# Dilated projections in natural token order, and the tiles of split products at one place modulo 256 bytes

## The chip, the cores and the metric

One Trainium2 chip; the kernel uses one of its cores. The metric is the device time of one execution in microseconds (us). A core has a matrix engine (PE; its weight loads, PEld, overlap its matmuls), a vector engine (DVE), an activation engine (ACT), a general engine (POOL) and a sync engine (SP) that issues every DMA of this kernel in order. On-chip memory is SBUF; matmuls write to PSUM.

## The reference, cut to what matters

Two networks run in sequence on 512 tokens of 1024 features in float32. The first is a mixer with two gated linear attentions followed by a PEER layer: top-k retrieval over 16384 experts, computed here densely as `gelu(u x)`, gates, and a product with `v`. The second has two layers; each is half a feed-forward block, a mixer, and another half:

```
swiglu_half: h = rms_norm(x, g);  (silu(h @ w_gate) * (h @ w_up)) @ w_down       # 1024 -> 2816 -> 1024
ab mixer:    z = rms_norm(x) @ ab_w_in; concat(mla_mixer(z), dilated_mixer(z)) @ ab_w_out
dilated_mixer(z): for g, (w, d) in enumerate(((128, 1), (512, 4), (2048, 16))):  # 4 heads of 64 per group
    q, k = qk_norm(zq_g), qk_norm(zk_g);  v = zv_g
    # to_res: tokens r, r+d, r+2d, ... form a sequence of their own
    o_g, lse_g = banded_attention(to_res(q), to_res(k), to_res(v), w // d + 1, bias, dist_scale=d)
  out = sum_g softmax_g(lse_g) * o_g
```

Groups 1 and 2 attend within residue classes of the token index (the kernel uses four classes for both; for `d = 16` its bias table masks what is not in the same class of 16).

## The kernel before, in words

Activations `x` lie feature-major: eight tiles of 128 features x 512 tokens. Nearly every large product is a *split product*. Both operands are split into a rounded high part and a low remainder in fp32r, and three matmuls accumulate high*high, high*low, low*high (`mm3`, L248 to L251). Weights are streamed: SP loads a `wst` tile of 128 x 1024 (four buffers), ACT writes the high part `whi`, DVE the low part `wlo` (`gran`, L213; three buffers of each). In feature-major products the weight block is the stationary operand and 512 tokens of the activation split are the moving one: names `gu` (gate and up), `dn` (down), `ua` and `qa` (PEER), `pacc` (PEER output), `fl`, `br`, `wo`, `mo`. In token-major products (`pj`, `vps`, `gps`) it is the other way round: 128 tokens of the activation split are stationary and 256 weight columns move (`project`, L1145).

The split activations are `xgh`/`xgl` in the second network, `hfh`/`hfl` into `dn`, `ph`/`pl` into `ua` and `qa`, `ag` into `pacc`, `mth`/`mtl` into `mo` of the ab mixer, `mt` into `mo` of the other mixer. Where a tile starts follows from the sizes of what was put in its pool before it; sizes are rounded to 32 bytes.

**ab mixer** (about 3009 to 3370 us). `mixer_ab` (L1194) makes twelve half projections F0 to F11: q, k, v of groups 1 and 2, each over 1024 x 256 weights, each half with two blocks of 128 tokens. Each block is 24 matmuls, so groups 1 and 2 have 6 x 4 x 24 = 576. Their tokens are taken with step 4, `s.st4 = [slice(i, 512, 4) ...]` (L1200), so that block `i` holds residue class `i`. The F pieces stand between the steps of `mla` (L1218): T0 to T7 (project, normalise and rotate one token block for four heads: PE `qb`, `kvb`, then ACT, POOL, DVE on tile `mx`, then PE transposes) and U0 to U7 (attention units: PE `lg`, DVE and ACT softmax, PE `tr`, `ob`). Then `dilated` (L1338): H0 to H2 normalise q and k of a group on DVE and transpose them (`dqT`, `dkT`, evicted by ACT), D are the attention units, E the projections of group 0 in natural order, O the output product `mo`. A scheduler fixes each engine's order when the program is built; the written order is its starting point.

Of the kernel before, what the change touches and what calls it, by code (L numbers as in the profile page):

```python
# [9 lines left out]
F32 = mybir.dt.float32  # L10
F32R = mybir.dt.float32r
F16 = mybir.dt.float16
I32 = mybir.dt.int32
# [140 lines left out]
    return {k: np.ascontiguousarray(v) for k, v in out.items()}  # L154


class Net:
    SQT = ("P", 2), ("L", 4)

    def __init__(s, ctx, tc, A, out, upto=None, dbg=None):  # L160
        s.ctx, s.tc, s.nc, s.A, s.out = ctx, tc, tc.nc, A, out
        s.upto, s.dbg = upto, dbg or {}
        s.hi_dve = False
        s.unnormed = False
        s.WB, s.NST = 3, 4
        nc = s.nc
        s.V, s.S, s.G, s.T = nc.vector, nc.scalar, nc.gpsimd, nc.tensor
        s.c = ctx.enter_context(tc.tile_pool(name="consts", bufs=1, reuse_waits="tile"))
        s.wp = ctx.enter_context(tc.tile_pool(name="weights", bufs=1, reuse_waits="tile"))
        s.dr = ctx.enter_context(tc.tile_pool(name="dram", bufs=1, space=DRAM))  # L170
        s.consts()

# [26 lines left out]
    def consts(s):  # L199
        c, V, G, A = s.c, s.V, s.G, s.A  # L200
        s.ones = c.tile([128, 128], F32, name="ones")
        V.memset(s.ones[:], 1.0)
        ii = c.tile([128, 128], I32, name="ii")
        G.iota(ii[:], pattern=[[1, 128]], base=0, channel_multiplier=-1)
        s.ident = c.tile([128, 128], F32, name="ident")
        s.ts(s.ident[:], ii[:], 0.0, None, ALU.is_equal)

        s.shift = c.tile([128, 128], F32, name="shift")
        s.ts(s.shift[:], ii[:], -1.0, None, ALU.is_equal)
        s.vecs = c.tile([128, 72], F32, name="vecs")  # L210
        s.load(s.vecs[:], A["vecs"])

    def gran(s, src):  # L213

# [140 lines left out]
    def first(s):  # L355
        tc, A, c = s.tc, s.A, s.c
        s.ysp = s.dr.tile([16, 128, 512], F32, name="ysp")
        with ExitStack() as es:
            s.ps = es.enter_context(s.psum(3, 1))
            hp = es.enter_context(tc.tile_pool(name="hpool", bufs=1, reuse_waits="tile"))  # L360
            with ExitStack() as e1:
                p = e1.enter_context(tc.tile_pool(name="adap", bufs=1, reuse_waits="tile"))
                s.ada_first(p, hp)()
            s.sgp = es.enter_context(tc.tile_pool(name="sgp", bufs=1, reuse_waits="tile"))
            with ExitStack() as e1:
                wk = e1.enter_context(tc.tile_pool(name="gla", bufs=1, reuse_waits="tile"))
                s.gla_setup(wk)
                for j in range(4):
                    s.hg_pair(wk, j)
                    if j == 0:  # L370
                        s.bias_skew()
                for h in range(4):
                    s.gla_head(wk, h)
                sgs = [s.merge_gate(m) for m in range(2)]
            mp = es.enter_context(tc.tile_pool(name="ymp", bufs=1, reuse_waits="tile"))
            with ExitStack() as e1:
                ym = s.merge(e1.enter_context(tc.tile_pool(name="merge", bufs=1, reuse_waits="tile")), mp, sgs)
            s.xp = s.ctx.enter_context(tc.tile_pool(name="xres", bufs=1, side="right", reuse_waits="tile"))
            s.mix_out(ym)

# [392 lines left out]
    def peer(s):  # L773
        tc, A = s.tc, s.A

        s.gd = [s.dr.tile([32, 128, 512], F32, name=f"gd{q}") for q in range(4)]
        s.ad = s.dr.tile([128, 128, 512], F32, name="ad")
        acc = s.sumsq_w(s.x)
        with tc.tile_pool(name="peer", bufs=1, reuse_waits="tile") as p:
            s.peer_u(p, acc)  # L780
            s.peer_v(p)

# [216 lines left out]
    def norm_in(s, gain):  # L999

        if not hasattr(s, "sb"):

            s.sb = s.ctx.enter_context(s.tc.tile_pool(name="second", bufs=1, reuse_waits="tile"))
        return [s.split(s.sb, s.x[k][:], "xg", 8, scale=gain[:, k:k + 1]) for k in range(8)]

    def norm_rs(s, p, views):
# [25 lines left out]
    def ffn(s, l, f):  # L1032
        A = s.A
        wgu, wd = A[f"wgu{l}{f}"], A[f"wd{l}{f}"]
        with ExitStack() as es:
            s.ps = es.enter_context(s.psum(6, 1))
            col = (24 if f == 1 else 56) + 8 * l
            gain = s.vecs[:, col:col + 8]
            if s.unnormed:
                s.tt(gain, gain, s.vecs[:, 16:24], ALU.mult)  # L1040
            xg = s.norm_in(gain)
            p = es.enter_context(s.tc.tile_pool(name="ffn", bufs=1, reuse_waits="tile"))
            nat = [slice(128 * i, 128 * i + 128) for i in range(4)]
            if s.unnormed:
                Rb = s.norm_twice(p, nat)
            else:
                Rb = s.bcast(p, s.norm_rs(p, nat))
            for half in range(2):
                H = []
                for m in range(11):  # L1050
                    pp = []
                    for e in range(2):
                        a = s.mm_ps("gu")
                        s.prod(a[:], s.gran(wgu[11 * half + m, e]), xg)
                        pp.append(a)
# [138 lines left out]
    def mixer_ab(s):  # L1194
        with ExitStack() as es:
            s.ps = es.enter_context(s.psum(3, 2))
            xg = s.norm_in(s.vecs[:, 40:48])
            p = es.enter_context(s.tc.tile_pool(name="ab", bufs=1, reuse_waits="tile"))
            s.nat = [slice(128 * i, 128 * i + 128) for i in range(4)]
            s.st4 = [slice(i, 512, 4) for i in range(4)]  # L1200
            R = s.norm_rs(p, s.nat + s.st4)
            mixed = p.tile([128, 4, 768], F32, name="mixed")
            s.dx = {}
            fill = [f for g in (1, 2) for n in range(3) for f in s.dil_proj(p, xg, R, g, n)]
# [5 lines left out]
    def dil_proj(s, p, xg, R, g, n):  # L1210

        def dst(i):
            if (g, n) not in s.dx:
                s.dx[g, n] = p.tile([128, 4, 4, 64], F32, tag="dx", bufs=6, name="dx")
            return s.dx[g, n][:, i].rearrange("p h d -> p (h d)")
        return s.halves(s.A["ab_d"][3 * g + n], xg, s.st4 if g else s.nat, R[:, 4:8] if g else R[:, 0:4], 256, dst)

    def mla(s, p, up, xg, R, mixed, fill):  # L1218
        A, V = s.A, s.V
# [22 lines left out]

        cm = p.tile([128, 512], F32, name="cm")
        V.memset(cm[:, :384], 0.0)
        gtm = p.tile([128, 128], I32, name="gtm")
        s.G.iota(gtm[:], pattern=[[1, 128]], base=0, channel_multiplier=-1)
        s.ts(cm[:, 384:], gtm[:], 0.0, BIG, ALU.is_gt, ALU.mult)

        ss = p.tile([128, 4, 2], F32, name="ss2")
        for i in range(4):  # L1250
# [72 lines left out]
        for n in order[order.index("Z") + 1:]:  # L1323
            pc[n]()

    def qk_heads(s, p, x, R_, nh, gain, neg, dst):


        for i in range(4):
# [3 lines left out]
            s.tt(x[:, i], x[:, i], r[:, :, None].to_broadcast([128, nh, 64]), ALU.mult)  # L1333
        for j in range(nh // 2):
            pt = s.transpose4([x[:, i, 2 * j:2 * j + 2, :].rearrange("p h d -> p (h d)") for i in range(4)])
            s.act(dst[j][:], pt[:], AF.Copy, scale=gain)

    def dilated(s, p, up, xg, R, mixed):  # L1338
        A, V = s.A, s.V
        hg = p.tile([128, 8], F32, name="hdg")  # L1340
        s.load(hg[:], A["hd_g"])
        perm = s.dr.tile([2, 512, 272], F32, name="perm")
        bias = [s.bias_tile(p, f"dil{g}") for g in range(3)]
        mt = [s.to_feat(p, mixed, k) for k in range(4)]
# [2 lines left out]
        def heads(g):  # L1347
            qT = [p.tile([128, 512], F32, tag="dqT", bufs=4, name="dqT") for _ in range(2)]
            kT = [p.tile([128, 512], F32, tag="dkT", bufs=4, name="dkT") for _ in range(2)]
            s.qk_heads(up, s.dx[g, 0], None, 4, hg[:, 0:1], -0.125, qT)  # L1350
            s.qk_heads(up, s.dx[g, 1], None, 4, hg[:, 1:2], None, kT)
            return qT, kT

        def units(g, i, qT, kT):
# [67 lines left out]
    def mixer_cd(s):  # L1422
        A = s.A
        with ExitStack() as es:
# [3 lines left out]
            nat = [slice(128 * i, 128 * i + 128) for i in range(4)]  # L1428
            R = s.norm_rs(p, nat)
            mixed = p.tile([128, 4, 1024], F32, name="mixed")  # L1430
            hg = p.tile([128, 8], F32, name="hdg")
            s.load(hg[:], A["hd_g"])
            flat = lambda t, i: t[:, i].rearrange("p h d -> p (h d)")

            def proj(n, t):
# [294 lines left out]
```

## Time and profile before

| | us |
|---|---|
| median of 3 runs (4804.04 to 4808.37) | 4805.89 |
| the profiled execution | 4807.03 |
| its span on the core | 4805.3 |
| PE busy in the span | 4691.8 |

The stages of the span: first mixer to 1014 us, PEER `ua` 1026 to 1918 and `pacc` 1918 to 2636, feed-forward halves 2638 to 3009, ab mixer to about 3370, two more halves to 4099, the other mixer to about 4430, the last half to 4805. A matmul's shown duration is longer than its step to the next one, since matmuls are pipelined: the step is read from starts. A busy share says nothing of how long each step is.

### The profile page before, as it was taken

The numbers are of one execution on the slowest core, as the hardware profiler recorded it, in microseconds if no ns is written. First come the engines' busy times: TensorE is split into PE (matmuls) and PEld (weight loads), VectorE is DVE, ScalarE is ACT, GpSimd is POOL, SyncE is SP. The second block draws the span as 40 slices with busy tenths as digits, with TensorE's granted clock in tenths as the row PEclk, the third lists the DMA queues.
The fourth block names the chain that finished last, engine by engine and source line by source line (L and its number), as shares of the span: only waits on it lengthen the run. The fifth ranks groups of instructions, "written<-read, shape, count | busy, mean of one in ns | idle before, by whom it ended". The sixth has DMA issues, their size and how long they took to land.

```text
span 4805.3 us, 61237 instructions
## 1 busy us (share of the span) xinstructions
PE 4691.8 (98%) x23805; PEld 3874.1 (81%) x23805; DVE 2535.3 (53%) x5117; ACT 1753.1 (36%) x3150; POOL 228.6 (5%) x204
## 2 busy tenths in 40 slices
PE   7999998999999999999999999999999999999999
PEld 5898886878888887888887888988788888966887
DVE  4655555568866553444445634356544544555443
ACT  3444344232345444222223323345323323354322
POOL 1000000000000000000000100010100100000100
PEclk8999899999999999999999999999999999999999
DMA  7222113433356667666665233211333333211332
GB/s 209 66 64 70 53 53 103 147 123 126 121 169 195 178 193 215 187 188 187 190 187 168 86 98 89 68 34 51 116 98 96 93 96 97 80 40 42 95 98 84
DMA packets 320655, 559.17 MB, mean 116 GB/s; under 512 B 153883, under 2 KB 163995, under 8 KB 320364
## 3 DMA queue, kind: packets, MB, share of 16 engines
q1 hardware_dynamic: 320364, 555.26, 38.5%
q8 instruction: 186, 3.05, 0.3%
q14 instruction: 105, 0.86, 0.1%
HBM read 480.58 MB, written 80.62 MB: 117 GB/s over the span
## 4 chain that ended last, share of the span: by engine, by line
PE 93%; DVE 2%; ACT 2%; DMA 2%; issue 1%; SPq 0%; DVEq 0%; ACTq 0%
PE gu L250 7%; PE gu L251 7%; PE gu L249 7%; PE ua L249 5%; PE ua L251 5%; PE ua L250 5%; PE pacc L249 5%; PE pacc L251 5%; PE pacc L250 5%; PE dn L251 3%; PE dn L250 3%; PE dn L249 3%; PE pj L249 2%; PE pj L250 2%; PE pj L251 2%; PE lg L1132 2%
## 5 line engine op out<-in xcount | busy, mean ns | idle before, releaser
L185 ACT ACTIVATE whi<-wst 128x1024 fp32r<-128x1024 f32 (+3 forms) x720 | 737.1, 1024 | 1529.9 <-issue 355.1
L188 DVE TENSOR_TENSOR wlo<-wst,whi 128x1024 fp32r<-128x1024 f32 (+3 forms) x720 | 945.1, 1313 | 615.9 <-ACT whi L185 592.8
L249 PE MATMUL gu<-xgh,whi 128*128 128x512 f32 x1408 | 549.4, 391 | 9.4 <-DVE x L188 7.2
L250 PE MATMUL gu<-xgl,whi 128*128 128x512 f32 x1408 | 550.0, 391 | 1.0 <-DVE xgl L197 1.0
L251 PE MATMUL gu<-xgh,wlo 128*128 128x512 f32 x1408 | 549.5, 390 | 0.0
L249 PE MATMUL ua<-ph,whi 128*128 128x512 f32 x1024 | 409.8, 400 | 2.2 <-ACT ph L185 2.2
L251 PE MATMUL ua<-ph,wlo 128*128 128x512 f32 x1024 | 407.0, 397 | 0.0
L250 PE MATMUL ua<-pl,whi 128*128 128x512 f32 x1024 | 406.4, 397 | 0.0
L249 PE MATMUL pacc<-ag,whi 128*128 128x512 f32 x1024 | 404.6, 395 | 0.7 <-ACT ge L185 0.7
L251 PE MATMUL pacc<-ag,wlo 128*128 128x512 f32 x1024 | 404.5, 395 | 0.0
L250 PE MATMUL pacc<-ag,whi 128*128 128x512 f32 x1024 | 404.5, 395 | 0.0
L188 DVE TENSOR_TENSOR t<-gu,Rb 128x512 f32<-128x512 f32 x176 | 120.7, 691 | 391.0 <-PE gu L251 384.5
L249 PEld LDWEIGHTS gu<-xgh,whi 128*128 128x128 f32 x1408 | 265.3, 188 | 66.0 <-issue 5.7
L250 PEld LDWEIGHTS gu<-xgl,whi 128*128 128x128 f32 x1408 | 265.2, 188 | 56.9 <-DVE xgl L197 1.9
L251 PEld LDWEIGHTS gu<-xgh,wlo 128*128 128x128 f32 x1408 | 265.3, 188 | 54.6
L249 PE MATMUL dn<-hfh,whi 128*128 128x512 f32 x704 | 277.6, 394 | 0.0
L251 PE MATMUL dn<-hfh,wlo 128*128 128x512 f32 x704 | 276.3, 394 | 0.0
L250 PE MATMUL dn<-hfl,whi 128*128 128x512 f32 x704 | 276.3, 394 | 0.0
L1061 POOL TENSOR_TENSOR t<-t,t 128x512 f32<-128x512 f32 x88 | 123.9, 1409 | 3108.2 <-ACT t L185 2116.2
L185 ACT ACTIVATE ag<-ga 128x512 fp32r<-128x512 f32 x128 | 80.9, 632 | 507.5 <-PE pacc L250 507.2
L249 PEld LDWEIGHTS pacc<-ag,whi 128*128 128x128 f32 x1024 | 191.9, 187 | 48.1 <-ACT ge L185 1.2
L251 PEld LDWEIGHTS pacc<-ag,wlo 128*128 128x128 f32 x1024 | 191.9, 187 | 47.0
(503 smaller groups left out, 9042.5 us busy)
## 6 DMA issues: line engine op xcount, KB each, us to landing
wst<-in_wgu_dram SPq DMA_DIRECT2D x176, 512.0 KB, 3.5
wst<-in_u_dram SPq DMA_DIRECT2D x128, 512.0 KB, 3.7
wst<-in_v_dram SPq DMA_DIRECT2D x128, 512.0 KB, 3.6
ad<-ge SPq DMA_DIRECT2D x128, 256.0 KB, 2.0
ga<-ad SPq DMA_DIRECT2D x128, 256.0 KB, 2.6
gd<-gst SPq DMA_DIRECT2D x32, 1024.0 KB, 11.4
gq<-gd SPq DMA_DIRECT2D x128, 256.0 KB, 3.0
wst<-in_wd_dram SPq DMA_DIRECT2D x64, 448.0 KB, 3.3
```

The lines of the kernel that those rows point to most:

```text
L185: s.S.activation(out, in_, f, **kw)
L188: s.V.tensor_tensor(out, a, b, op)
L249: s.T.matmul(ps, a[0], b[0], start=start, stop=False)
L250: s.T.matmul(ps, a[0], b[1], start=False, stop=False)
L251: s.T.matmul(ps, a[1], b[0], start=False, stop=stop)
L1061: s.G.tensor_tensor(u[:], u[:], t[:], ALU.mult)
L1132: s.T.matmul(lp[:, :n], q, k, start=True, stop=True)
```

## The change

**Order of tokens.** The projections of groups 1 and 2 now take 128 neighbouring tokens (`s.nat`) and the statistics of four token slices instead of eight. q and k are put into residue order when ACT evicts their transposes: it reads PSUM with a step of four elements. v is put into residue order by a round trip: `dx` is stored to the DRAM tile `vperm` and loaded back as four runs of 1 KB per partition.

**Places.** `Lines` wraps a tile pool and rounds each tile's size up to 128 or 256 bytes. Most pools with operands of split products are wrapped. Three small tiles go: `ii` borrows a weight buffer, `gtm` is written into `cm`, `hdg` becomes eight more columns of `vecs`, loaded at the start. In the built programs the tiles start here, in bytes modulo 256:

| operand | before | after |
|---|---|---|
| `whi`, `wlo` (weights); `xgh`, `xgl`; all activation splits of the first mixer; `mt` | 96 | 128 |
| `ph`, `pl` (`ua`, `qa`: 3456 matmuls) | 64 | 128 |
| `ag` (`pacc`: 3072) | 128 | 128 |
| `hfh`, `hfl` (`dn`: 2112) | 32, some 128 | 128 |
| `mth`, `mtl` (`mo` of the ab mixer: 144) | 0 | 128 |

Before, 8784 matmuls of these four rows have their operands at different places, and some 9800 at the same one (96 and 96).

```
class Lines:
    def tile(s, shape, dt, **kw):
        n, size = math.prod(shape[1:]), s.BYTES[dt]
        if n * size % s.unit == 0:
            return s.pool.tile(shape, dt, **kw)
        t = s.pool.tile([shape[0], -(-n * size // s.unit) * s.unit // size], dt, **kw)[:, :n]
        ...
-        s.wp = ctx.enter_context(tc.tile_pool(name="weights", bufs=1, reuse_waits="tile"))
+        s.wp = Lines(ctx.enter_context(tc.tile_pool(name="weights", bufs=1, reuse_waits="tile")))
...
-            s.st4 = [slice(i, 512, 4) for i in range(4)]
-            R = s.norm_rs(p, s.nat + s.st4)
+            R = s.norm_rs(p, s.nat)
+            s.vperm = s.dr.tile([2, 512, 256], F32, name="vperm")
...
-        return s.halves(s.A["ab_d"][3 * g + n], xg, s.st4 if g else s.nat, R[:, 4:8] if g else R[:, 0:4], 256, dst)
+        h = s.halves(s.A["ab_d"][3 * g + n], xg, s.nat, R, 256, dst)
+        if g == 0 or n < 2:
+            return h
+
+        def last():
+
+            h[1]()
+            x = s.dx[g, n][:].rearrange("p i h d -> p i (h d)")
+            s.store(s.vperm[g - 1].rearrange("(i p) c -> p i c", p=128), x)
+            s.load(x, s.vperm[g - 1].rearrange("(p r) c -> p r c", r=4))
+        return [h[0], last]
...
+            if residues:
+                s.act(dst[j][:].rearrange("p (r a) -> p r a", r=4), pt[:].rearrange("p (a r) -> p r a", r=4), AF.Copy, scale=gain)
```

The order of instructions on PE, DVE, ACT and POOL hardly changes (a few neighbours swap). Two places differ. On the SP queue, in the ab mixer before (`in_ab_d` are the dilated weights, `in_ab_o` the output weights, `b_dil` the bias tiles, `hdg` the gains):

```order
L175 DMA wst<-in_ab_d_dram 128x1024 x10
L175 DMA wst<-in_ab_o_dram 128x512
L175 DMA wst<-in_ab_d_dram 128x1024 x4
L175 DMA wst<-in_ab_o_dram 128x512
L175 DMA wst<-in_ab_d_dram 128x1024
L175 DMA hdg<-in_hd_g_dram 128x8
L175 DMA b_dil_26121<-sk_dil_1440 128x4x256
```

and now, the same stretch of the SP queue:

```order
L193 DMA wst<-in_ab_d_dram 128x1024 x10
L196 DMA vperm<-dx 128x4x256
L193 DMA wst<-in_ab_o_dram 128x512
L193 DMA dx<-vperm 128x1024
L193 DMA wst<-in_ab_d_dram 128x1024 x4
L196 DMA vperm<-dx 128x4x256
L193 DMA wst<-in_ab_o_dram 128x512
L193 DMA wst<-in_ab_d_dram 128x1024
L193 DMA dx<-vperm 128x1024
L193 DMA b_dil_26120<-sk_dil_1441 128x4x256
```

Each group's v is stored and loaded back, with one or two weight loads between; the bias tiles come behind the second load, and the load of `hdg` has gone to the start of the program.

On PE, between the first projections of the ab mixer, the statistics matmuls before:

```order
L249 MATMUL pj<-whi,xgh 128x256
L250 MATMUL pj<-wlo,xgh 128x256
L321 MATMUL st<-ones,acc 128x1 x8
L251 MATMUL pj<-whi,xgl 128x256
L249 MATMUL pj<-whi,xgh 128x256
```

and now:

```order
L268 MATMUL pj<-whi,xgh 128x256
L269 MATMUL pj<-wlo,xgh 128x256
L340 MATMUL st<-ones,acc 128x1 x4
L270 MATMUL pj<-whi,xgl 128x256
L268 MATMUL pj<-whi,xgh 128x256
```

Four of the eight go; the projections around them stand as they stood.

## Rows read from the trace of the kernel before

**Rows 1.** the page: span, part 1, part 4's shares of the chain

```profile
span 4805.3 us, 61237 instructions
PE 4691.8 (98%) x23805; PEld 3874.1 (81%) x23805; DVE 2535.3 (53%) x5117; ACT 1753.1 (36%) x3150; POOL 228.6 (5%) x204
PE 93%; DVE 2%; ACT 2%; DMA 2%; issue 1%; SPq 0%; DVEq 0%; ACTq 0%
```

**Rows 2.** windows of tiles `gu` and `dn`: window, length, PE busy (matmuls), granted clock

```profile
3917.82:4037.52 119.70, 119.70 (x528) 1.00 0.31 96
...
4037.52:4098.88 61.36, 61.36 (x263) 1.00 0.33 95
```

**Rows 3.** windows of tiles `ua` and `pacc`, the same columns

```profile
1873.58:1918.46 44.88, 44.88 (x192) 1.00 0.93 271
...
1918.46:2636.03 717.57, 716.82 (x3071) 1.00 0.63 185
```

**Rows 4.** tile `mo`: count, shortest/median/longest ns, first and last start us

```profile
L249 PE MATMUL mo<-mt,whi x64: 389/393/774, 4273.6 to 4428.4; 128*128 128x512 f32 x64
L249 PE MATMUL mo<-mth,whi x48: 389/400/793, 3242.0 to 3366.5; 128*128 128x512 f32 x48
```

**Rows 5.** timeline, PE: gate projection `gz`, whose stationary operand has 24 columns

```profile
4182.04 0.39 PE L249 MATMUL gz<-xgh,whi 128*24 128x512 f32 x1
...
4184.57 0.39 PE L251 MATMUL gz<-xgh,wlo 128*24 128x512 f32 x1
```

**Rows 6.** projections `pj`: timeline (start us, us, line, form), then the tile's weight loads

```profile
3049.30 0.40 PE L249 MATMUL pj<-whi,xgh 128*128 128x256 f32 x1
...
3060.50 0.38 PE L351 MATMUL tr<-ident,za 128*128 128x128 f32 x2
...
L249 PEld LDWEIGHTS pj<-whi,xgh x16: 329/329/329, 3049.2 to 3059.7; 128*128 128x128 f32 x16
```

**Rows 7.** `pj`, 3020 to 3025.8: window (length, PE, PEld busy, count), weight loads

```profile
3020.00:3025.80 5.80, 5.76 (x48) 5.76 (x49) 0.37 (x1) 1.96 (x5) 0.00 (x0) 1.00 0.02 3
...
L249 PEld LDWEIGHTS pj<-whi,xgh x17: 186/192/192, 3020.0 to 3025.8; 128*128 128x128 f32 x17
```

**Rows 8.** timeline, ACT: one plain 128-column eviction

```profile
3187.05 0.28 ACT L185 ACTIVATE P<-tr 128x128 f32<-128x128 f32 x1 [3.37 <-PE tr L1138]
```

**Rows 9.** tile `dqT`: its ACT evictions from PSUM

```profile
L185 ACT ACTIVATE dqT<-tr,hdg x6: 678/684/692, 3247.1 to 3315.7; 128x512 f32<-128x512 f32 x6
```

**Rows 10.** tile `st`: statistics matmuls of this stage, from 3014 to 3018

```profile
L321 PE MATMUL st<-ones,acc x16: 168/310/372, 3014.4 to 3016.8; 128*128 128x1 f32 x16
```

**Rows 11.** windows: length, then PE, PEld, DVE, ACT, POOL busy us (count)

```profile
1100.00:1200.00 100.00, 99.33 (x453) 80.95 (x452) 84.82 (x349) 29.49 (x40) 0.00 (x0) 1.00 0.38 124
3029.00:3231.00 202.00, 200.26 (x981) 185.65 (x980) 91.19 (x303) 74.17 (x182) 28.23 (x41) 1.00 0.11 35
3216.79:3231.35 14.56, 14.56 (x67) 13.38 (x67) 7.14 (x34) 5.15 (x9) 2.41 (x3) 1.00 0.08 20
3231.00:3251.00 20.00, 17.70 (x133) 14.94 (x133) 19.71 (x107) 12.19 (x24) 3.87 (x6) 1.00 0.27 80
```

**Rows 12.** timeline: rope of step T2 on DVE and its transposes on PE

```profile
3126.18 0.42 DVE L188 TENSOR_TENSOR mx<-mx,rp 128x256 f32<-128x256 f32 x1
...
3131.45 1.03 PE L351 MATMUL tr<-ident,mx 128*96 128x128 f32 x8
```

**Rows 13.** timeline, DVE then PE: step T7, the weight split behind it, T7's transposes

```profile
3216.38 0.41 DVE L188 TENSOR_TENSOR mx<-mx,rp 128x256 f32<-128x256 f32 x1
...
3226.16 1.23 DVE L188 TENSOR_TENSOR wlo<-wst,whi 128x1024 fp32r<-128x1024 f32 x1 [5.68 <-ACT whi L185]
...
3226.04 1.03 PE L351 MATMUL tr<-ident,mx 128*96 128x128 f32 x8
```

**Rows 14.** DMA issues, 3000 to 3360 (KB, us to landing), then timeline, SP queue

```profile
b_dil<-sk_dil SPq DMA_DIRECT2D x1, 512.0 KB, 5.4
...
3227.41 0.33 SPq L175 DMA_DIRECT2D wst<-in_ab_o_dram  x1
```

More of the change, by code (lines that the diff above doesn't have):

```diff
@@ L154, in layout, with __init__, tile @@
     return {k: np.ascontiguousarray(v) for k, v in out.items()}
+class Lines:
+    BYTES = {F32: 4, F32R: 4, I32: 4, U32: 4, F16: 2}
+    def __init__(s, pool, lines=1):
+        s.pool, s.unit = pool, 128 * lines
+    def tile(s, shape, dt, **kw):
+        n, size = math.prod(shape[1:]), s.BYTES[dt]
+        if n * size % s.unit == 0:
+            return s.pool.tile(shape, dt, **kw)
+        t = s.pool.tile([shape[0], -(-n * size // s.unit) * s.unit // size], dt, **kw)[:, :n]
+        dims = "abcde"[:len(shape) - 1]
+        if len(dims) > 1:
+            t = t.rearrange(f"p ({' '.join(dims)}) -> p {' '.join(dims)}", **dict(zip(dims[1:], shape[2:])))
+        return t
 class Net:
@@ L167, in __init__ @@
         s.V, s.S, s.G, s.T = nc.vector, nc.scalar, nc.gpsimd, nc.tensor
-        s.c = ctx.enter_context(tc.tile_pool(name="consts", bufs=1, reuse_waits="tile"))
-        s.wp = ctx.enter_context(tc.tile_pool(name="weights", bufs=1, reuse_waits="tile"))
+        s.c = Lines(ctx.enter_context(tc.tile_pool(name="consts", bufs=1, reuse_waits="tile")), 2)
+        s.wp = Lines(ctx.enter_context(tc.tile_pool(name="weights", bufs=1, reuse_waits="tile")))
         s.dr = ctx.enter_context(tc.tile_pool(name="dram", bufs=1, space=DRAM))
@@ L202, in consts @@
         V.memset(s.ones[:], 1.0)
-        ii = c.tile([128, 128], I32, name="ii")
-        G.iota(ii[:], pattern=[[1, 128]], base=0, channel_multiplier=-1)
+        ii = s.wp.tile([128, 1024], F32, tag="wst", bufs=s.NST, name="ii")[:, :128].bitcast(I32)
+        G.iota(ii, pattern=[[1, 128]], base=0, channel_multiplier=-1)
         s.ident = c.tile([128, 128], F32, name="ident")
-        s.ts(s.ident[:], ii[:], 0.0, None, ALU.is_equal)
+        s.ts(s.ident[:], ii, 0.0, None, ALU.is_equal)
         s.shift = c.tile([128, 128], F32, name="shift")
-        s.ts(s.shift[:], ii[:], -1.0, None, ALU.is_equal)
-        s.vecs = c.tile([128, 72], F32, name="vecs")
-        s.load(s.vecs[:], A["vecs"])
+        s.ts(s.shift[:], ii, -1.0, None, ALU.is_equal)
+        s.vecs = c.tile([128, 80], F32, name="vecs")
+        s.load(s.vecs[:, :72], A["vecs"])
+        s.load(s.vecs[:, 72:], A["hd_g"])
     def gran(s, src):
@@ L359, in first @@
             s.ps = es.enter_context(s.psum(3, 1))
-            hp = es.enter_context(tc.tile_pool(name="hpool", bufs=1, reuse_waits="tile"))
+            hp = Lines(es.enter_context(tc.tile_pool(name="hpool", bufs=1, reuse_waits="tile")))
             with ExitStack() as e1:
@@ L363, in first @@
                 s.ada_first(p, hp)()
-            s.sgp = es.enter_context(tc.tile_pool(name="sgp", bufs=1, reuse_waits="tile"))
+            s.sgp = Lines(es.enter_context(tc.tile_pool(name="sgp", bufs=1, reuse_waits="tile")))
             with ExitStack() as e1:
@@ L374, in first @@
                 sgs = [s.merge_gate(m) for m in range(2)]
-            mp = es.enter_context(tc.tile_pool(name="ymp", bufs=1, reuse_waits="tile"))
+            mp = Lines(es.enter_context(tc.tile_pool(name="ymp", bufs=1, reuse_waits="tile")))
             with ExitStack() as e1:
-                ym = s.merge(e1.enter_context(tc.tile_pool(name="merge", bufs=1, reuse_waits="tile")), mp, sgs)
+                ym = s.merge(Lines(e1.enter_context(tc.tile_pool(name="merge", bufs=1, reuse_waits="tile"))), mp, sgs)
             s.xp = s.ctx.enter_context(tc.tile_pool(name="xres", bufs=1, side="right", reuse_waits="tile"))
@@ L779, in peer @@
         with tc.tile_pool(name="peer", bufs=1, reuse_waits="tile") as p:
+            p = Lines(p, 2)
             s.peer_u(p, acc)
@@ L1001, in norm_in @@
         if not hasattr(s, "sb"):
-            s.sb = s.ctx.enter_context(s.tc.tile_pool(name="second", bufs=1, reuse_waits="tile"))
+            s.sb = Lines(s.ctx.enter_context(s.tc.tile_pool(name="second", bufs=1, reuse_waits="tile")))
         return [s.split(s.sb, s.x[k][:], "xg", 8, scale=gain[:, k:k + 1]) for k in range(8)]
@@ L1041, in ffn @@
             xg = s.norm_in(gain)
-            p = es.enter_context(s.tc.tile_pool(name="ffn", bufs=1, reuse_waits="tile"))
+            p = Lines(es.enter_context(s.tc.tile_pool(name="ffn", bufs=1, reuse_waits="tile")), 2)
             nat = [slice(128 * i, 128 * i + 128) for i in range(4)]
@@ L1197, in mixer_ab @@
             xg = s.norm_in(s.vecs[:, 40:48])
-            p = es.enter_context(s.tc.tile_pool(name="ab", bufs=1, reuse_waits="tile"))
+            p = Lines(es.enter_context(s.tc.tile_pool(name="ab", bufs=1, reuse_waits="tile")))
             s.nat = [slice(128 * i, 128 * i + 128) for i in range(4)]
-            s.st4 = [slice(i, 512, 4) for i in range(4)]
-            R = s.norm_rs(p, s.nat + s.st4)
+            R = s.norm_rs(p, s.nat)
+            s.vperm = s.dr.tile([2, 512, 256], F32, name="vperm")
             mixed = p.tile([128, 4, 768], F32, name="mixed")
@@ L1244, in mla @@
         V.memset(cm[:, :384], 0.0)
-        gtm = p.tile([128, 128], I32, name="gtm")
-        s.G.iota(gtm[:], pattern=[[1, 128]], base=0, channel_multiplier=-1)
-        s.ts(cm[:, 384:], gtm[:], 0.0, BIG, ALU.is_gt, ALU.mult)
+        gtm = cm[:, 384:].bitcast(I32)
+        s.G.iota(gtm, pattern=[[1, 128]], base=0, channel_multiplier=-1)
+        s.ts(cm[:, 384:], gtm, 0.0, BIG, ALU.is_gt, ALU.mult)
         ss = p.tile([128, 4, 2], F32, name="ss2")
@@ L1324, in mla, with qk_heads @@
             pc[n]()
-    def qk_heads(s, p, x, R_, nh, gain, neg, dst):
+    def qk_heads(s, p, x, R_, nh, gain, neg, dst, residues=False):
         for i in range(4):
@@ L1335, in qk_heads @@
             pt = s.transpose4([x[:, i, 2 * j:2 * j + 2, :].rearrange("p h d -> p (h d)") for i in range(4)])
-            s.act(dst[j][:], pt[:], AF.Copy, scale=gain)
+            if residues:
+                s.act(dst[j][:].rearrange("p (r a) -> p r a", r=4), pt[:].rearrange("p (a r) -> p r a", r=4), AF.Copy, scale=gain)
+            else:
+                s.act(dst[j][:], pt[:], AF.Copy, scale=gain)
     def dilated(s, p, up, xg, R, mixed):
         A, V = s.A, s.V
-        hg = p.tile([128, 8], F32, name="hdg")
-        s.load(hg[:], A["hd_g"])
+        hg = s.vecs[:, 72:]
         perm = s.dr.tile([2, 512, 272], F32, name="perm")
@@ L1349, in heads @@
             kT = [p.tile([128, 512], F32, tag="dkT", bufs=4, name="dkT") for _ in range(2)]
-            s.qk_heads(up, s.dx[g, 0], None, 4, hg[:, 0:1], -0.125, qT)
-            s.qk_heads(up, s.dx[g, 1], None, 4, hg[:, 1:2], None, kT)
+            s.qk_heads(up, s.dx[g, 0], None, 4, hg[:, 0:1], -0.125, qT, g > 0)
+            s.qk_heads(up, s.dx[g, 1], None, 4, hg[:, 1:2], None, kT, g > 0)
             return qT, kT
@@ L1430, in mixer_cd @@
             mixed = p.tile([128, 4, 1024], F32, name="mixed")
-            hg = p.tile([128, 8], F32, name="hdg")
-            s.load(hg[:], A["hd_g"])
+            hg = s.vecs[:, 72:]
             flat = lambda t, i: t[:, i].rearrange("p h d -> p (h d)")
```

## The prediction

> **What bounds the kernel now.** I read the page first. The matrix engine is busy 98% of the span, and 93% of the chain that ended last is on it [rows 1]; DVE has 53%, ACT 36%. So the span is the number of matmuls times the step from one to the next. A busy share doesn't tell whether that step is long or short, so I went on to stretches in which PE never paused and divided their length by their count. In a feed-forward half, `gu` takes 119.70 us for 528 matmuls, 226.7 ns each, and `dn`, which follows at once with the same shape and the same granted clock of 1.00, takes 61.36 us for 263, 233.3 ns [rows 2]. `ua` needs 233.8 ns and `pacc` 233.7 [rows 3]. Two products on one source line with one shape differ too: the median record of `mo` is 393 ns in one mixer and 400 in the other [rows 4]. What separates the two groups is the table of places: the operands of `gu` and of the 393 ns `mo` both start at 96 modulo 256, those of `dn`, `ua`, `pacc` and the 400 ns `mo` at two different places. That is what the tile rounding acts on.
>
> Then the ab mixer. The projections of groups 1 and 2, whose 128 stationary tokens are taken with step 4, need 11.20 us for 48 matmuls of 256 columns: 233.3 ns, with a weight load of 329 ns [rows 6]. The same product with neighbouring tokens does 48 in 5.76 us, 120.0 ns, weight load 192 ns [rows 7]. The weight load grows by 137 ns with the step of four, the matmul's own columns are the same, and the step grows by 113 ns. PE is busy in 200.3 of the 202 us from 3029 to 3231, while DVE has 91 and ACT 74 [rows 11], so time taken from these matmuls is time of the stage until a wait takes its place.
>
> **The change part by part.** *Natural order.* 576 matmuls go from 233.3 to 120.0 ns: 576 x 113.3 ns = 65.3 us less of PE. Eight of sixteen statistics records go, of which 16 start within 2.4 us [rows 10]: about 0.16 us each, 1.3 us less.
>
> *Places.* The 8784 matmuls with different places come to one place, those of `dn` for instance from 233.3 to 226.7: 8784 x 6.6 ns = 58.0 us less (`ua` 22.8, `pacc` 20.3, `dn` 13.9, `mo` 1.0). The 0.4 ns by which `ua` and `pacc` lie above `dn` I leave where they are. No run shows a pair at (128, 128); the bounds are nothing gained and, if the other matmuls lose what these gain, a loss (rivals).
>
> *New waits in the ab mixer.* The projections are fill between steps of the attention, so each step's results are wanted earlier. In T2 the rope on DVE ends at 3126.60 and PE transposes at 3131.45, 4.85 us later [rows 12]; of the 48 projection matmuls that stand between, 5.4 us are saved: a wait of 0.6. In T7 DVE is done at 3216.79 and PE comes at 3226.04 [rows 13], 9.25 us of slack against 89 x 113.3 ns = 10.1: 0.9. After T7, DVE itself is late: it has 7.14 us of work in the 14.56 us up to the first unit of the stage with the bias tiles [rows 11], which PE would allow 10.1 us sooner, at 3221.3; DVE can be there at 3216.79 + 7.14 = 3223.9, 2.7 us late. From 3231 to 3251 it works 19.71 of 20 us [rows 11], so it can't catch up. One thing softens this: the 5.68 us for which DVE sat before `wlo` was a wait for `whi` [rows 13], whose buffer comes free with the projections that now run faster. That is 4.2 us; with the steps not looked at, I take 6. Below, nothing (if the attention moves up along with the projections); above, see the first rival. Behind a waiting transpose PE's whole queue waits.
>
> *Evictions with step 4.* Eight evictions of q and k to residue order replace eight of 684 ns [rows 9]. If step 4 costs nothing, 0; if it costs what four separate evictions of 128 columns cost, 4 x 0.28 us [rows 8], 0.44 more each: 3.5 us. ACT is busy 12 of 20 us there [rows 11]; I take 1, since the row of the same size is the nearest. The Trainium skill ("SBUF — State Buffer", Door 1: The DMA port swizzle) speaks against this edit: it says that PSUM is read well only in runs of two float32 and that other patterns are slow, for matmuls above all. No row before shows ACT reading PSUM with step 4; by that rule the upper end, 3.5, would stand, or more.
>
> *Round trip of `v`.* Two stores and two loads of 512 KB join the SP queue. The store waits for the last eviction of `dx`, and the queue behind it waits too: weight loads, and at the end the bias tiles. A transfer of 512 KB in 1 KB pieces lands in 5.4 us; the next weight load in the queue goes out at 3227.41 [rows 14], when PE is at T7's transposes, and what it brings is for the output product, later than 3242 [rows 4]. The `v` of a group is first read some units after its q and k are normalised and transposed. So I count nothing. If that cover is gone, it is twice out and back, 4 x 5.4 = 21.6 us.
>
> *The rest.* The load of the gains moves to the start, where the SP queue feeds a cold start: one issue, 0.33 us as in [rows 14]. In `ua` DVE is busy 84.8 of 100 us [rows 11]; a step shorter by 2.8% makes that 87.3, still under PE: 1 us for moments in which it isn't. If that cover failed altogether, the 22.8 of `ua` would be lost.
>
> Sum on the profiled execution: 4807.0 - 65.3 - 1.3 - 58.0 + 6 + 1 + 0.3 + 1 = 4690.7. It ran 1.1 above the median of 4805.89, so I predict 4690, 2.4% less.
>
> **The rivals.** *The attention doesn't move.* If its chain on DVE and ACT keeps its own pace, each of the eight T steps gives back the 5.4 us that its 48 matmuls saved: 43.5 in place of 6, so up to 4727. For it: T2's slack is under 5.4. Against it: DVE is free for more than half of the stage [rows 11], and the one long idle time in [rows 13] ends on work that moves up.
>
> *Place is not what separates them.* Then `dn` is slow for something else that it shares with `ua` and `pacc`, and the 58.0 isn't gained: 4748. Against it: [rows 2] and [rows 4] hold everything else equal that I can see. The Trainium skill ("TensorE: Matmul & The Clock Gate", Step-by-step: what each phase is for) supports this rival: PE reads weights and moving data through two independent ports, so loading the next weights costs the running matmul nothing, and by that where the two lie should not matter. The trace doesn't bear it out as it stands: 6.6 ns separate [rows 2].
>
> *96 itself is the good place.* Every fast pair that the trace has is (96, 96). If 128 is a bad place for the weights or the data, equal or not, the some 9,800 matmuls that are fast today go to 233.3 and so may the 576: 9,800 x 6.6 + 576 x 6.6 = 68.5 lost and 58.0 not gained, 4816, slower by 0.2%. It decides from 8,800 such matmuls on, since all the rest of the sum is -58.3. Against it: `gz`, with its moving data at 96 and its weights at many places, does 11 steps from 4182.04 to 4184.57 [rows 5], 230.0 ns, so a moving operand at 96 alone isn't enough, and neither does a moving operand at 0, 32, 64 or 128 seem to differ from the others in [rows 3] and [rows 4]; but weights at 96 are in all of these, so it isn't excluded.
>
> *Round places are better still.* 512 columns at 2.4 GHz are 213.3 ns, so 13.4 ns of overhead remain in a step of 226.7. If tiles on a 128-byte boundary shed another 6.6 on some 18,600 matmuls, 123 us more go: 4567. Nothing in the trace speaks for it: places 0 and 128 have been tried by one operand and were no quicker.
>
> **How the numbers follow.** The forecast, 0.68, with its own range from 4679 (no waits, and the 0.4 ns of `ua` and `pacc` gone too) to 4704 (the upper ends of waits and evictions, part of `ua` lost). The attention doesn't move, 0.12, 4704 to 4727. Place means nothing, 0.10, 4748. 96 is the good place, 0.04, 4816. Round places better still, 0.06, 4567. The range from 4665 to 4750 leaves out the last two and little of the others. What a measurement can tell from no change is about 0.2%, 9.6 us: only the 4816 is on the other side of it, so faster has 0.95, slower 0.03, and 0.02 is left for between.
>
> **What would show it.** Places: in the halves `gu` and `dn` should both step by 226.7 ns, and `ua` and `pacc` by about 227; `dn` at 233 is the second rival, `gu` at 233 the third, anything under 225 the fourth. Natural order: all `pj` weight loads at 192 ns and 48 matmuls in 5.76 us. Waits: PE idle before T2's and T7's transposes under 1 us each, about 3 near the first bias unit, 6 in all from 3020 to 3310; 40 would be the first rival. Evictions of `dqT` from 684 to 1120 ns. PE idle until the second load of `v` would show that the round trip isn't covered. I am wrong if the steps stay or if the ab mixer shortens by less than 40 us.

## The result, and the profile after

The changed kernel takes 4689.83 us (median of 4 runs, 4689.27 to 4692.11) against 4804.97 for the one before: ratio 0.976, interval 0.9743 to 0.9777. 4690 was predicted. The page of the profile after gives the span, the busy time of each engine, and the shares of the chain:

```profile
span 4687.9 us, 61227 instructions
...
PE 4570.9 (98%) x23797; PEld 3809.1 (81%) x23797; DVE 2533.1 (54%) x5117; ACT 1752.7 (37%) x3150; POOL 227.9 (5%) x204
...
PE 92%; DVE 3%; DMA 2%; ACT 2%; issue 1%; SPq 0%; POOL 0%; DVEq 0%; ACTq 0%; POOLq 0%
```

PE still sets the end, as in [rows 1]; it has 121 us less to do and DVE and ACT have what they had. Windows of the tiles `gu`, `dn`, `ua` and `pacc` after (window, length, PE busy and matmuls, granted clock, then DMA share and GB/s):

```profile
3803.59:3923.05 119.46, 119.45 (x528) 1.00 0.31 96
...
3923.28:3982.89 59.61, 59.61 (x264) 1.00 0.32 96
...
1853.03:1896.66 43.63, 43.63 (x192) 1.00 0.93 278
...
1896.66:2593.84 697.18, 696.40 (x3072) 1.00 0.64 190
```

A step is the time from the start of one matmul to the start of the next; where a window ends at the start of its last matmul, it holds one step less than matmuls. `gu` takes 119.46 / 527 steps = 226.7 ns, as before. `dn` now takes 59.61 / 263 = 226.7, where [rows 2] had 233.3; `ua` 43.63 / 192 = 227.2 and `pacc` 697.18 / 3071 = 227.0, where [rows 3] had 233.8 and 233.7. Places that are equal modulo 256 are enough: in the built program the weights start at 384 modulo 512 and `ph` at 128, and `ua` is quick all the same. The tile `mo`, columns as in [rows 4]:

```profile
L268 PE MATMUL mo<-mt,whi x64: 389/393/796, 4157.5 to 4314.6; 128*128 128x512 f32 x64
...
L268 PE MATMUL mo<-mth,whi x48: 387/393/795, 3133.9 to 3256.8; 128*128 128x512 f32 x48
```

Both mixers' `mo` now have the same median. The projections of group 1 on PE (start us, us, line, form), first and last of 28 that follow one another without a pause, and then the tile's weight loads over the kernel:

```profile
3011.62 0.28 PE L268 MATMUL pj<-whi,xgh 128*128 128x256 f32 x1
...
3014.86 0.28 PE L268 MATMUL pj<-whi,xgh 128*128 128x256 f32 x1
```

```profile
L268 PEld LDWEIGHTS pj<-whi,xgh x608: 186/192/245, 2963.6 to 4118.3; 128*128 128x128 f32 x152
```

Before, the same line read

```profile
L249 PEld LDWEIGHTS pj<-whi,xgh x608: 186/192/334, 3009.2 to 4234.4; 128*128 128x128 f32 x152
```

27 steps in 3.24 us are 120.0 ns, against 233.3 in [rows 6]; the longest weight load is down from 334 to 245 ns.

A total hides where it came from, so I cut the span at the first matmul of each stage, from the starts in the trace (us; the two right columns are the first two experiments below):

| stage | before | after | places only | order only |
|---|---|---|---|---|
| first mixer, to the first `ua` | 1025.71 | 1023.56 | 1027.84 | 1025.37 |
| `ua`, `qa` | 892.75 | 873.09 | 873.34 | 892.21 |
| `pacc` | 719.49 | 699.10 | 699.10 | 719.50 |
| two feed-forward halves | 371.51 | 368.11 | 368.13 | 369.93 |
| ab mixer | 359.78 | 295.72 | 359.38 | 294.78 |
| two halves | 729.88 | 723.52 | 721.95 | 730.64 |
| other mixer | 335.48 | 337.65 | 334.46 | 334.40 |
| last halves, to the last `dn` | 366.67 | 362.91 | 362.60 | 366.18 |

64.1 us come from the ab mixer, 19.7 from `ua` and `qa`, 20.4 from `pacc`, 13.5 from the halves. Two stages that the change hardly touches moved too, by -2.1 and +2.2. Windows over all engines (length, PE, PEld, DVE, ACT, POOL busy, then granted clock) show what differs in them: before, the whole ab mixer, a stretch near its end, a piece of the other mixer, and a piece of the first mixer:

```profile
3009.46:3369.24 359.78, 349.67 (x1994) 313.96 (x1992) 196.19 (x806) 161.81 (x431) 38.03 (x56) 0.99 0.17 52
...
3350.67:3357.50 6.83, 6.02 (x15) 4.46 (x16) 1.57 (x3) 1.08 (x2) 0.00 (x0) 0.50 0.00 0
...
4271.50:4288.00 16.50, 16.50 (x80) 12.36 (x78) 7.50 (x32) 8.69 (x35) 0.00 (x0) 0.87 0.06 16
...
127.00:143.00 16.00, 13.35 (x54) 11.48 (x55) 9.14 (x22) 6.25 (x13) 0.00 (x0) 0.57 0.11 34
```

and after, the stretch of the first bias units, then the same four:

```profile
3121.00:3142.00 21.00, 17.60 (x128) 14.44 (x127) 20.96 (x108) 11.12 (x22) 4.66 (x7) 1.00 0.39 124
...
2963.87:3259.59 295.72, 282.09 (x1985) 245.58 (x1984) 195.84 (x806) 161.33 (x431) 38.79 (x56) 0.99 0.22 71
...
3243.27:3246.68 3.41, 3.17 (x8) 2.50 (x9) 1.29 (x2) 0.67 (x2) 0.00 (x0) 0.50 0.00 0
...
4155.50:4172.00 16.50, 16.50 (x68) 12.49 (x67) 6.34 (x28) 7.21 (x31) 0.00 (x0) 0.72 0.05 17
...
127.00:143.00 16.00, 14.22 (x91) 11.40 (x90) 11.83 (x26) 8.92 (x14) 0.00 (x0) 1.00 0.22 67
```

Near 4156 after, the granted clock was 0.72 where it had been 0.87 before; from 127 to 143 it was 1.00 where it had been 0.57. The clock is at its half level (1.2 GHz, 0.50 in these rows) in short stretches, and where they fall differs from one execution to the next. The ab mixer has 6.8 us of it before and 3.4 after, so up to 1.7 of its 64.1 us (an estimate, half of the difference) are the clock's and not the change's.

### The profile page after: what moved, and what is told of

Read it like the earlier page. It is cut to its first block, busy times and chain, and to the rows that moved or that the text cites. A ratio compares the mean times of both kernels' runs of the same rounds, so it can differ in the third digit from the quotient of the medians.

```text
span 4687.9 us, 61227 instructions
## 1 busy us (share of the span) xinstructions
PE 4570.9 (98%) x23797; PEld 3809.1 (81%) x23797; DVE 2533.1 (54%) x5117; ACT 1752.7 (37%) x3150; POOL 227.9 (5%) x204
## 4 chain that ended last, share of the span: by engine, by line
PE 92%; DVE 3%; DMA 2%; ACT 2%; issue 1%; SPq 0%; POOL 0%; DVEq 0%; ACTq 0%; POOLq 0%
PE gu L268 7%; PE gu L269 7%; PE gu L270 7%; PE ua L268 5%; PE ua L270 5%; PE ua L269 5%; PE pacc L268 5%; PE pacc L269 5%; PE pacc L270 5%; PE dn L269 3%; PE dn L270 3%; PE dn L268 3%; PE lg L1152 2%; PE ob L1163 2%; PE fl L268 2%; PE fl L269 2%
## 5 line engine op out<-in xcount | busy, mean ns | idle before, releaser
L268 PE MATMUL pacc<-ag,whi 128*128 128x512 f32 x1024 | 398.5, 389 | 0.8 <-ACT ge L203 0.8
L269 PE MATMUL pacc<-ag,whi 128*128 128x512 f32 x1024 | 398.3, 389 | 0.0
L268 PEld LDWEIGHTS ua<-ph,whi 128*128 128x128 f32 x1024 | 192.6, 188 | 40.7 <-ACT ph L203 2.5
```

What stands on the lines that cost most here:

```text
L268: s.T.matmul(ps, a[0], b[0], start=start, stop=False)
L269: s.T.matmul(ps, a[0], b[1], start=False, stop=False)
```

## The experiments

**The two parts apart.** `places_only` is the changed kernel with the old order of tokens:

```
-            R = s.norm_rs(p, s.nat)
-            s.vperm = s.dr.tile([2, 512, 256], F32, name="vperm")
+            s.st4 = [slice(i, 512, 4) for i in range(4)]
+            R = s.norm_rs(p, s.nat + s.st4)
...
-        h = s.halves(s.A["ab_d"][3 * g + n], xg, s.nat, R, 256, dst)
...
+        return s.halves(s.A["ab_d"][3 * g + n], xg, s.st4 if g else s.nat, R[:, 4:8] if g else R[:, 0:4], 256, dst)
```

> The changed kernel with the old order of tokens (projections of groups 1 and 2 with step 4, eight statistics slices, no residue evictions, no round trip of v); the places stay at 128. My theory: the places by themselves are worth 19.7 us in ua and qa, 20.4 in pacc, 14 in dn and 1 in mo as the trace after shows them, so 4805 - 55 = 4750, from 4745 to 4754, and every step of 512 columns is 226.7 ns. Rival, place is not what separates the steps and the order of the program or of DMA traffic did it: 4805 and dn at 233.3 ns.

4748.1 us (4743.64 to 4752.6) against 4807.44 in the same session, ratio 0.9875, interval 0.9859 to 0.9892. `dn`, `pacc` and `qa` step by 226.7 ns (steps that show no pause), and by stage (table) 55.6 us come from `ua`, `pacc`, the halves and the ab mixer's `mo`. That is as my theory said; the rival, that something other than place separates the steps, is out.

`order_only` leaves the sizes as they are:

```
-        if n * size % s.unit == 0:
+        if True:
             return s.pool.tile(shape, dt, **kw)
```

> The changed kernel without the rounding of tile sizes: the operands of ua, qa, pacc and dn start 32 or 64 bytes away from the weights modulo 256 (mo of the ab mixer happens to stay at one place with them). My theory: natural order alone saves what the ab mixer lost from the trace before to the trace after, 64.1 us, so 4805 - 64 = 4741, from 4737 to 4745; dn, ua, pacc step by 233.3 ns. Rival, the two parts share a gain (for instance because waits in the ab mixer hide part of either): then this one is nearer 4690 + 40 = 4730 and the sum of both gains is above 116.

4737.43 us (4736.15 to 4738.99), ratio 0.9855, interval 0.9839 to 0.9872. `dn`, `pacc` and `qa` stay at 233.3 ns, `ua` at 233.0. The total is 4 us lower than I expected, and the two gains, 59.3 and 70.0, are together more than the 115.1 of the changed kernel. Taken alone that is the rival's sign, but the table says otherwise: in the ab mixer the parts give 0.4 and 65.0 and both give 64.1, in `ua` 19.4 and 0.5 against 19.7. They add up within 1.6 us in each stage on which they act. The rest lies in the first and the other mixer, which both have stretches at the low clock (there the parts and the whole differ by up to 4.3 us), and between the sessions.

**Which places.** `sweepA` and `sweepB` put a pad ahead of the tiles of a stage, so that its moving operand starts some bytes further than the weights (the distance). `sweepA` does it for `hf` in the four halves and, by 32 bytes, for `ph`, `pl` and `ag`:

```
+            pad = p.tile([128, 4], F32, name="padp")      # sweepA alone
+            s.V.memset(pad[:], 0.0)
...
+            off = (32, 64, 128, 192)[2 * l + f - 1]      # sweepB: (96, 160, 224, 0)
+            if off:
+                pad = p.pool.tile([128, off // 4], F32, name="padf")
+                s.V.memset(pad[:], 0.0)
...
-        s.vecs = c.tile([128, 80], F32, name="vecs")
+        s.vecs = c.pool.tile([128, 80], F32, name="vecs")   # sweepB: all tiles 64 bytes on, at 192
```

> The changed kernel with its weights at 128 and some of the moving operands moved away: the four feed-forward halves' hf by 32, 64, 128 and 192 bytes in this order (dn), ph, pl and ag by 32 (ua, qa, pacc). Theory 'one place modulo 256': each of these steps is 233.3 ns, also the one at 128, and the kernel is 8640 x 6.67 = 57.6 us longer, about 4747. Rival 'every operand on a 128-byte boundary': the half at 128 bytes' distance steps by 226.7 ns, the others by 233.3. Rival 'the weights' place alone': all stay at 226.7 and the kernel at 4690.

4744.92 us. Windows of tile `dn`, one in each half, distance 32, 64, 128, 192 bytes (263 steps each):

```profile
2945.16:3006.53 61.37, 61.37 (x264) 1.00 0.30 90
...
3428.86:3489.07 60.21, 60.21 (x263) 1.00 0.31 98
...
3791.08:3852.44 61.36, 61.36 (x264) 1.00 0.31 97
...
4496.23:4557.60 61.37, 61.37 (x263) 1.00 0.32 97
```

These are 233.3, 228.9, 233.3, 233.3 ns, and `pacc` at 32 takes 719.49 us again, as before the change. So 128 bytes apart is as slow as any: the rival of the 128-byte boundary is out, and so is the one by the weights' place alone. The 228.9 at 64 was not expected.

> The changed kernel with every operand of split products at 192 in place of 128, but hf of the feed-forward halves at 96, 160, 224 and 0 bytes from the weights (the last half at one place with them). Theory 'one place modulo 256, whichever': gu, ua, pacc and the last dn step by 226.7 ns, the first three dn by 233.3; 1584 x 6.67 = 10.6 us longer than 4690, about 4700. Rival 'a 128-byte boundary counts': 192 is off it, so gu, ua and pacc go to 233.3 and the kernel to 4690 + some 18,600 x 6.67 = 4814.

4702.56 us. A window of `gu`, then four of `dn` (distance 96, 160, 224, 0):

```profile
4517.28:4636.73 119.45, 119.45 (x527) 1.00 0.30 96
...
2905.59:2966.97 61.38, 61.38 (x263) 1.00 0.29 90
...
3387.09:3448.70 61.61, 61.61 (x263) 1.00 0.31 96
...
3752.09:3813.45 61.36, 61.36 (x263) 1.00 0.32 97
...
4636.96:4696.57 59.61, 59.61 (x263) 1.00 0.25 80
```

`gu` at (192, 192) steps by 119.45 / 527 = 226.7, the three displaced `dn` by 233.4, 234.3 and 233.3, the last by 226.7. `pacc` at (192, 192) is at 697 us again. So it is not 96 or 128 that is good, but that both operands are at the same place.

**How exact.** `fine` shifts the weights of 64 pieces of the down projection inside their buffer:

```
+            if m == 896:
+                s.turn = getattr(s, 'turn', -1) + 1
+                a, b = 2 * (s.turn % 32), 2 * (s.turn % 32)
+            hi, lo = hi[:, a:a + m], lo[:, b:b + m]
```

> The changed kernel, in which the split weights of 64 pieces of the down projection (7 blocks of 128 columns each) start 0, 8, 16, ... 248 bytes further in their buffer, two pieces for each distance; the moving operand stays at 128. Theory 'the same place to the byte, modulo 256': 42 matmuls of dn at each distance from 8 to 248 step by 233 ns (229 at 192, as in the sweep before), only distance 0 by 226.7; 1302 x 6.6 = 8.6 us more, 4698. Rival 'the same 32 or 64 bytes suffice': distances 8 to 24 (or 56) step by 226.7, the rest by 233. A third possibility: some distance is quicker than 226.7, which would be a better place than the changed kernel's.

4693.62 us. Mean steps of 40 matmuls at each distance: 226.7 at 16, 144 and 240, 226.8 at 120; 229 to 232 at 8, 24, 80, 152, 176, 184, 192, 200, 208 and 232; 232 to 234 at the other seventeen. So both named theories are wrong as they stand: 8 bytes apart is slower, 16 apart is not. (Weights 192 further are the moving operand 64 further, the 228.9 of `sweepA`.) None was quicker than 226.6. Why just these distances are quick, no run shows. `four` asks whether the four were chance, with one of them in all of a half (its edit against `fine`):

```
-                a, b = 2 * (s.turn % 32), 2 * (s.turn % 32)
+                a, b = (4, 30, 36, 60)[s.turn // 16], (4, 30, 36, 60)[s.turn // 16]
```

> The changed kernel, in which the split weights of the 64 pieces of the down projection start 16, 120, 144 and 240 bytes further, one distance in each of the four halves (336 matmuls each). These four were as quick as distance 0 in the sweep by 8 bytes, where each had 40 matmuls. Theory 'one place modulo 256 is enough, but not needed': all four halves step by 226.7 ns again, 4690. Rival 'the fast distances of the sweep were chance, of where in time a piece began': three or four of them are at 231 to 233.3, and the kernel up to 1344 x 6.67 = 9.0 us longer, 4699.

Windows of `dn`, distance 16, 120, 144, 240 (two thirds of the matmuls displaced):

```profile
2729.66:2789.27 59.61, 59.61 (x263) 1.00 0.33 98
...
3388.64:3448.25 59.61, 59.61 (x263) 1.00 0.33 99
...
3749.55:3809.17 59.62, 59.62 (x264) 1.00 0.32 98
...
4449.69:4509.31 59.62, 59.62 (x264) 1.00 0.33 98
```

All are at 226.7. Equal places are enough, and not needed. The kernel took 4694.8 us; the 5 us above the changed kernel lie ahead of the first `ua`, where the two programs do the same work.

**Which matmul pays.** `low_only` and `low16` displace the low weights alone, by 32 and by 16 bytes (edit against `fine`):

```
-                a, b = 2 * (s.turn % 32), 2 * (s.turn % 32)
+                a, b = 0, 8                                   # low16: 0, 4
```

> The changed kernel, in which only the low part of the weights of those 64 pieces starts 32 bytes further, so that of each three matmuls (high weights, high weights, low weights) only the third has its operands at two places. Theory 'a matmul is held up by the load of the next one's weights': the step after the second matmul, under which the low weights are loaded, is 233.3 ns, the other two are 226.7. Rival 'a matmul is slow by its own two operands': the step after the third is 233.3. Either way 448 x 6.67 = 3.0 us more, 4693.

4698.25 us. A window of `dn`, two thirds of it displaced:

```profile
2723.41:2784.11 60.70, 60.70 (x264) 1.00 0.32 97
```

That is 230.8 ns over all. In the displaced pieces the three steps are 232.4, 239.0 and 228.5 ns (means of 383 groups): 699.9 together, as much as when all three differ, 20 in place of the 6.7 expected. The longest is the one under which the low weights load, as my theory had it, but it is not the only one, so both theories failed on the price.

> The changed kernel, in which only the low part of the weights of those 64 pieces starts 16 bytes further (with 32 bytes all three matmuls of a group became slower, 20.0 ns for the three). Theory 'a distance that is fast by itself is fast in a mixture': no change, 680 ns for three matmuls and 4690. Rival 'what costs is that neighbouring weight loads differ in place': about 20 ns more for three, 448 x 20 = 9.0 us, 4699.

4692.24 us, and the same window:

```profile
2727.45:2787.06 59.61, 59.61 (x264) 1.00 0.33 98
```

That is 226.7, or 680.0 ns for three. Weights that alternate between two places cost nothing at this distance, which is a quick one by itself; the rival is out. Why 32 bytes in one of three matmuls slow all three stays open.

**The round trip of `v`.** `no_trip` is the changed kernel without `s.store(s.vperm...)` and `s.load(x, s.vperm...)`; it leaves the reordering of `v` out.

> The changed kernel without the two stores and two loads of v, which leaves v in natural order (not what the reference computes). Theory 'the round trip is covered': the ab mixer takes 295.7 us as in the changed kernel, within 1 us (up to 1.7 more or less by where the clock steps down), and the kernel 4690. Rival 'the SP queue or the late v holds something up': it is shorter by part of 4 x 5.4 us, up to 21.

4695.86 us. The ab mixer, as the window above:

```profile
2969.82:3269.16 299.34, 285.09 (x1986) 248.12 (x1984) 195.79 (x806) 161.43 (x431) 38.81 (x56) 0.98 0.20 62
```

That is 299.34 us against 295.72, 3.6 more and not within the 1.7 that I allowed; 3.0 of it is PE's work time at a lower mean clock (0.98 for 0.99). Three stretches of 3.4 us at half clock fall into this stage (from 2979.73, 3222.08 and 3252.80), against one in the changed kernel; two more of them are worth up to 3.4 us, half of their length, by estimate. Up to the first `mo` it took 172.1 against 170.0, with one such stretch and none in the other. The rival wanted the stage shorter; nothing was gained by leaving the trip out, so it is covered.

**The step of the tokens.** `steps` takes group 1 with step 2 and group 2 with step 4:

```
+        tk = {0: s.nat, 1: [slice(256 * (i // 2) + i % 2, 256 * (i // 2) + 256, 2) for i in range(4)], 2: [slice(i, 512, 4) for i in range(4)]}[g]
-        h = s.halves(s.A["ab_d"][3 * g + n], xg, s.nat, R, 256, dst)
+        h = s.halves(s.A["ab_d"][3 * g + n], xg, tk, R, 256, dst)
```

> The changed kernel, in which the stationary tokens of group 1 are taken with step 2 and those of group 2 with step 4 (the attention then sees them in another order than the reference's). Theory 'the weight load of a projection is as long as the pieces of 16 bytes that it reads': step 4 reads 128 of them and 48 matmuls need 11.2 us as before, step 2 reads 64 and the matmuls step by 120 to 158 ns (at 120 if the load then fits under the matmul). Rival 'any step over 1 is one read per element': step 2 is at 233.3 ns too. The ab mixer gets 288 x 113.3 = 32.6 us longer by group 2, and by group 1 between 0 and 32.6: 4722 to 4755.

4722.85 us, and the ab mixer 33.8 us longer. The tile's weight loads with step 2 and with step 4 (count, shortest/median/longest ns):

```profile
L268 PEld LDWEIGHTS pj<-whi,xgh x31: 193/195/200, 2990.1 to 3000.9; 128*128 128x128 f32 x31
...
L268 PEld LDWEIGHTS pj<-whi,xgh x16: 310/330/335, 3041.4 to 3052.8; 128*128 128x128 f32 x16
```

Step 2 loads in 195 ns, 3 more than neighbouring tokens, and its matmuls keep a step of 120 (median of 281). Step 4 loads in 330 and its matmuls step by 233. That is my theory's lower end; the rival is out.

No run points to a version that beats the changed kernel: no place was quicker than its own, and no order of tokens loads quicker than the natural one.

## Why the prediction was right, and where it was not

The steps that carried it held. *What bounds*: PE. *Natural order*: 576 steps went from 233.3 to 120.0, the 65.3 us; the stage got 64.1 shorter. *Places*: the steps fell to 226.7, and the experiments took the second, third and fourth rival out: place matters, 96 is not special, and no place was better.

The total agrees more closely than its terms do. The ab mixer was counted 65.3 + 1.3 + 1.0 - 6 - 1 = 60.6 us shorter and got 64.1, `ua` and `qa` were counted 21.8 and got 19.7; the two misses have opposite signs, and that the total came within 1 us is luck. The terms one by one:

- *`ua`*: 22.8 less 1 was counted, 19.7 came. The steps between two `ua` matmuls that show no pause fell by 5.6 ns (233.0 to 227.4), not 6.6: after, 327 of 2871 take 230 to 237 ns, with nothing that PE waits for. The trace shows where they are: 239 of them are among the second to sixth step behind a group of short `g` matmuls (128 columns), whose results ACT evicts to `gst` at that time. Those steps took 230.9 ns in the mean before and take 231.2 now, so place gives them nothing; all other steps went from 233.3 to 226.9. I had named DVE as the risk. Whether the `g` matmuls, the evictions or something else there slows these steps stays open. `pacc` (20.3 counted, 20.4) and the halves (13.9, 13.5) came as counted.
- *New waits*: 6 counted. PE's time not busy in the ab mixer went from 359.78 - 349.67 = 10.1 to 295.72 - 282.09 = 13.6, 3.5 more. The rows of T2, T7 and the first bias unit after, each time DVE's row ahead of PE's:

```profile
3048.01 0.42 DVE L206 TENSOR_TENSOR mx<-mx,rp 128x256 f32<-128x256 f32 x1
...
3048.49 1.08 PE L370 MATMUL tr<-ident,mx 128*96 128x128 f32 x8 [0.61 <-DVE mx L206]
...
3115.48 0.41 DVE L206 TENSOR_TENSOR mx<-mx,rp 128x256 f32<-128x256 f32 x1
...
3116.75 1.03 PE L370 MATMUL tr<-ident,mx 128*96 128x128 f32 x8
...
3123.70 0.68 DVE L1154 CUSTOM_DVE_ANT_0 L<-lg,cm 128x512 f32<-128x512 f32 x1
...
3124.44 1.12 PE L1152 MATMUL lg<-mkT,mqT 96*128 96x512 f32 x2 [0.68 <-DVE lm L1154]
```

In T2 PE waits 0.61 us, as worked out. In T7 it waits for nothing: DVE's rope came 100.9 us earlier than in [rows 13] and PE 109.3, so 8.4 of the slack went, not 10.1, and 0.86 is left. At the first bias unit DVE's softmax is late and PE waits 0.68 where 2.7 were counted; from 3121 to 3142 DVE is busy 20.96 of 21 us (first row of the windows after). The list of what PE waited for in the stage (us, times, longest) has these three that were not there before or were shorter:

```profile
PE pj L269 <- DVE wlo L206: 0.9, 1, 0.9
...
PE lg L1152 <- DVE lm L1154: 0.9, 2, 0.7
...
PE tr L370 <- DVE mx L206: 0.6, 1, 0.6
```

So the attention moved up with the projections, nearly all of it; the first rival, which had 43.5 us of waits, is out.

- *Evictions*: 1 counted, nothing came:

```profile
L203 ACT ACTIVATE dqT<-tr,vecs x6: 677/684/690, 3139.1 to 3207.5; 128x512 f32<-128x512 f32 x6
```

684 ns as in [rows 9], with four of the six rows read at step 4 from PSUM. Neither the upper end nor the rule of the Trainium skill quoted there ("SBUF — State Buffer", Door 1: The DMA port swizzle) shows in ACT's time; for matmuls, of which it speaks above all, no run here shows it.
- *Statistics*: 1.3 counted. The eight records hold the projections up from 2968.78 to 2969.59 us, 0.81, where the sixteen took 2.68; that is 1.9 less.
- *Round trip*: nothing counted, nothing came. Issues on the SP queue after (start us, us):

```profile
3032.17 0.38 SPq L196 DMA_DIRECT2D vperm<-dx  x1
...
3034.41 0.33 SPq L193 DMA_DIRECT2D wst<-in_ab_o_dram  x1
...
3036.71 0.33 SPq L193 DMA_DIRECT2D dx<-vperm  x1
```

The store goes out at 3032.17 and the load of `v` 4.5 us later. The second load goes out at 3124.24 and takes some 4 us to land; the first product that reads any of these tiles starts at 3144.7. `no_trip` shows the same.
- *Clock*: not in the sum. The first mixer got 2.1 us shorter and the other one 2.2 longer, with the low stretches at other times. They cancel here; in the experiments that ran once they don't. In the changed kernel and six experiments with the same first mixer (`fine`, `four`, `low_only`, `low16`, `no_trip`, `steps`), it took from 1022.2 to 1029.3 us up to the first `ua`, so a difference of 5 us between two totals says nothing unless a stage shows it.

What the prediction quoted of the Trainium skill on PE's two read ports ("TensorE: Matmul & The Clock Gate", Step-by-step: what each phase is for) doesn't hold as it was read there: by that reading place should be free, and 6.6 ns over a 226.7 ns step hang on it.

## What to carry to other kernels

A busy engine can still be slow at each step: divide the length of a stretch without pauses by its count, compare tiles of one shape, and where they differ look at what the profile doesn't show, such as where the operands start. A stationary operand whose elements lie some way apart can cost much: here taking every second token was free under matmuls of 256 columns (120 ns each), and every fourth nearly doubled them (233 ns). Compare single executions stage by stage, since the same work moved a total by some 5 us here, and the stretches at the low clock fell differently.

## What the runs showed of the hardware that was not expected

A split-product matmul of 512 columns steps by 226.7 ns at some places of its operands and by 233.3 at most others. Equal places modulo 256 give the lower value at 96, 128 and 192; weights 16, 120, 144 or 240 bytes further give it too, 8 and 24 give 231, seventeen of the 32 distances tried 232 to 234. One displaced weight tile in three, 32 bytes off, costs the upper value for all three matmuls; 16 bytes off it costs nothing. Behind a group of `g` matmuls, five steps of `ua` take 231 ns in the mean, with the places of before and of after. ACT reads 512 float32 of PSUM with step 4 in the time of a plain read, 684 ns. A weight load of 128 columns takes 192 ns with step 1, 195 with step 2, 330 with step 4. The Trainium skill ("SBUF — State Buffer", Specifications (TRN2)) states lines of 16 bytes that want two hits each for full bandwidth; step 2 in float32 has two in a line and step 4 one, and the trace agrees, 195 against 330 ns.
